# Attention scores with 64 contracted rows: the two row halves by turns, kept together, and one mask product for a whole PSUM bank

## Chip, cores and metric

The kernel runs on one core of a Trainium2 chip. A core has five engines that matter here: TensorE (PE, matrix products, with its weight loads PEld), VectorE (DVE), ScalarE (ACT), GpSimd (POOL) and SyncE (SP, which issues the DMAs). The metric is the device time of one execution in microseconds (us). Lower is better.

## The reference, cut to what matters

Two decoder layers over 256 tokens of width 1024 in float32. Layer 0 mixes differential attention and a Mamba-2 scan, then a SwiGLU. Layer 1 mixes native sparse attention (NSA) and multi-head latent attention (MLA), then eight routed SwiGLU experts of which each token takes two. The change touches the three places where causal attention scores are made:

```python
# layer 0, differential attention: 4 heads, 2 components of 64 dimensions each
sc = jnp.einsum('bqhcd,bkhcd->bhcqk', q_blk, k) * d ** -0.5
p = softmax(where(causal, sc, NEG_INF)); attn = p[:, :, 0] - lam_full * p[:, :, 1]
# layer 1, MLA: 4 heads, each 128 dimensions without and 64 with rotary position
q_full = concatenate([q_nope, q_rope]); k_full = concatenate([k_nope, k_r])
o = causal_attention_blocked(q_full, k_full, v, 192 ** -0.5)
# layer 1, NSA: 2 groups of 4 heads, 64 dimensions; selected and window branch
s_s = einsum('bqgrd,bgqkd->bgrqk', q_blk, k_sel) * scale    # all 4 blocks are selected here
s_w = einsum('bqgrd,bkgd->bgrqk', q_blk, k_win) * scale     # the window covers all tokens
```

Queries are taken in two blocks of 128 (b = 0, 1). Block b sees K = 128 (b + 1) keys, of which the last 128 are masked causally.

## The kernel before

**Stages.** Layer 0's projections, scan, attention and output projection run until some 140 us, its SwiGLU until some 320 us, layer 1's projections and attentions until some 475 us, the routing until some 490 us, and the experts until the end. In the experts 1 MB weight tiles come in through the tiles `raw`, `xres`, `xg`, `more` and `fl`; weights that take part in a split product are divided into a high part `wh` and a rest `wl` (ACT or DVE makes `wh`, DVE makes `wl`), and `mm3` multiplies by them in three products (the lines 498, 499 and 500 of the profile).

**What sets the order.** All code outside the SwiGLU's and the experts' loops is recorded by `Recorder` and put into an order by a list scheduler: `flush` runs it with four settings (`WAYS`) and keeps the order with the shortest planned end. Each recorded operation has an engine (or two to choose from, `flex` and `either`), a planned duration (`pe_cost` and its like), and predecessors by the regions that it reads and writes. A new duration or a new operation anywhere can thus move every other operation of the same flush. There are two flushes: layer 0 up to the first SwiGLU chunk, and from the last SwiGLU chunk to the first experts' gather. The loops of the SwiGLU and of the experts are written out in program order. Recorded operations stand in the profile under the line of the proxy's call, 312 (317 in the loops).

**Scores.** A score tile `ps` is one PSUM bank of 512 columns (`pa()`, a ring of eight). `sp[0]` and `sp[1]` hold two 256-column halves each (`i`, or `br` in NSA). The operands of component or group 0 lie in partitions 0 to 63, those of component or group 1 in 64 to 127, so the products for `sp[0]` use the upper half of TensorE's rows and those for `sp[1]` the lower half. These products are plain float32, and each shows in the trace as two passes (two weight loads, two matmuls). `mask_add` adds the causal mask as a product of `identr` and `negmr`, both fp32r, one pass of 128 columns for each of the two halves of a bank. Then `softmax_exp` takes a maximum of the bank on DVE (`nm`) and two exponentials on ACT, `probs_T` transposes the result on PE, and products with the values follow. Ahead of the change every one of these products is an operation of its own, which the scheduler places freely.

In differential attention there are 16 such 64-row products (8 for each query block), in MLA 8 (the rotary part, after a 128-row product for the rest), in NSA 32.

Of the kernel before, what the change touches and what calls it, by code (L numbers as in the profile page):

```python
# [2 lines left out]

# [1 line left out]

# [14 lines left out]
P = 128  # L20
# [33 lines left out]
BIG = 4  # L54
HALFP = 64
LAG = 3
LATE, AFTER, HALF = 1, 2, 3
EXPLN = "natural_log_exp_and_others"
SILU = "silu_and_others"
# [8 lines left out]
class Recorder:  # L68
# [14 lines left out]
            (0.035, 2.357, 18.415, 0.5, 15.484, 17.49))  # L83

    def __init__(self):
        self.on, self.late = False, 0
        self.rings, self.ring_of, self.held = {}, {}, {}
        self.reset()

# [20 lines left out]
    def add(self, alts, outs, ins, table=None):  # L110
        o = _Op()
        o.i, o.alts, o.preds, o.succs, o.allocs = len(self.ops), alts, set(), [], []
        o.late = self.late
        rr = [r for r in map(self.region, ins) if r is not None]
        ww = [r for r in map(self.region, outs) if r is not None]
        o.touch = {r[0] for r in rr + ww}
        o.start = max((t for r in rr for lo, hi, t in self.when.get(r[0], ()) if lo < r[4] and r[3] < hi), default=0.0)
        for n in o.touch:
            if n in self.ring_of and n not in self.wr and n not in self.held:
                o.allocs.append(n)  # L120
                self.first[n] = o.i
            elif n in self.first:
                o.preds.add(self.first[n])
            self.wr.setdefault(n, [])
            self.rd.setdefault(n, [])
        pe = alts[0][0] == "PE"

        def hits(lst, r):

            for j, q, qpe in lst:  # L130
                if (q[1] < r[2] and r[1] < q[2] and q[3] < r[4] and r[3] < q[4]) or (pe and qpe and r[5]):
                    yield j

        for r in rr:
            o.preds.update(hits(self.wr[r[0]], r))
        for r in ww:
            o.preds.update(hits(self.wr[r[0]], r))
            o.preds.update(hits(self.rd[r[0]], r))
        for r in rr:
            self.rd[r[0]].append((o.i, r, pe))  # L140
        for r in ww:
            self.wr[r[0]].append((o.i, r, pe))
        if table == "load":
            o.preds.update(self.since)
            self.since = []
            if self.fence is not None:
                o.preds.add(self.fence)
            self.fence = o.i
        elif table == "use":
            if self.fence is not None:  # L150
                o.preds.add(self.fence)
            self.since.append(o.i)
        self.ops.append(o)

    def hold(self, tiles):
        self.held.update({ap.tensor.name: True for ap in tiles if ap.tensor.name in self.ring_of})
# [147 lines left out]
class Proxy:  # L304
# [9 lines left out]
    def __getattr__(self, fn):  # L314
        def call(*args, table=None, **kw):
            if not self.rec.on:
                return getattr(self.eng, fn)(*args, **kw)  # L317
            outs, ins = operands(args, kw)
            self.rec.add([self.alt(fn, args, kw)], outs, ins, table)
        return call  # L320


# [53 lines left out]
def kernel(ctx: ExitStack, tc: tile.TileContext, a, out: bass.AP):  # L376
    nc = tc.nc
    rec = Recorder()
# [127 lines left out]
    def mmx(o, l, r, start, stop):  # L506
        T.matmul(o, l, r, start=start, stop=stop, skip_group_check=True)
# [103 lines left out]
            flex(dstT[:, :, b * P:(b + 1) * P], tp.rearrange("p (i t) -> p i t", i=4))  # L611
        return f

    def mask_add(ps):
        mmx(ps, identr, negmr, False, True)

    def softmax_exp(s2, pr, sums):

# [6 lines left out]
    def v2(t, K):  # L625
        return t.rearrange("p (c k) -> p c k", c=2)[:, :, :K]
# [336 lines left out]
    for b in range(2):  # L963
        K = P * (b + 1)
        ops = pa()
        for hp_ in range(2):
            sp = [pa() for c in range(2)]
            for i in range(2):
                for c in range(2):
                    mmx(sp[c][:, i * 256:i * 256 + K], qT[c * 64:(c + 1) * 64, 2 * hp_ + i, b * P:(b + 1) * P],  # L970
                        kT[c * 64:(c + 1) * 64, 2 * hp_ + i, 0:K], i == 0, False)
            prs, sms = [], []
            for c in range(2):
                for i in range(2):
                    mask_add(sp[c][:, i * 256 + b * P:i * 256 + K])
                pr = v2(tw(), K)
                sums = small([P, 2], "sums")
                softmax_exp(v2(sp[c], K), pr, sums)
                prs.append(pr)
                sms.append(sums)  # L980
                V.reciprocal(sums, sums)
            V.tensor_scalar(sms[1], sms[1], nlam, None, op0=OP.mult)
            for i in range(2):
                V.tensor_scalar(prs[1][:, i, :], prs[1][:, i, :], sms[1][:, i:i + 1], None, op0=OP.mult)
                V.scalar_tensor_tensor(prs[0][:, i, :], prs[0][:, i, :], sms[0][:, i:i + 1], prs[1][:, i, :],
                                       op0=OP.mult, op1=OP.add)
            pt = probs_T(prs[0], b)
            for i in range(2):
                h = 2 * hp_ + i
                for j in range(b + 1):  # L990
                    o = (i * (b + 1) + j) * P
                    mmx(ops[:, h * P:(h + 1) * P], pt[:, o:o + P], v_sb[:, j, h * P:(h + 1) * P], j == 0, j == b)
            cs = slice(hp_ * 256, (hp_ + 1) * 256)
            on = norm_heads(ops[:, cs].rearrange("p (h d) -> p h d", d=P), 2, P)
            mx = mixt[b][0][:, cs]
            V.tensor_tensor(mx.rearrange("p (h d) -> p h d", d=P), on, bc(gsub[:, None, :], [P, 2, P]), OP.mult)
            mp.feat(0, b, 2 * hp_, mx)
# [213 lines left out]
    for b in range(2):  # L1211
        K = P * (b + 1)
        ts = slice(b * P, (b + 1) * P)
        ops = pa()
        sp = [pa() for c in range(2)]
        for i in range(2):
            for c in range(2):
                h = 2 * i + c
                o = sp[c][:, i * 256:i * 256 + K]
                mmx(o, qnT[:, h, ts], knT[:, h, 0:K], i == 0, False)  # L1220
                mmx(o, qrT[64 * c:64 * c + 64, i, ts], krT[64 * c:64 * c + 64, 0:K], False, False)
                mask_add(sp[c][:, i * 256 + b * P:i * 256 + K])
        sums = small([P, 2, 2], "sums4")
        for c in range(2):
            pr = v2(tw(), K)
            softmax_exp(v2(sp[c], K), pr, sums[:, :, c])
            pt = probs_T(pr, b)
            for i in range(2):
                h = 2 * i + c
                for j in range(b + 1):  # L1230
                    o = (i * (b + 1) + j) * P
                    mmx(ops[:, h * P:(h + 1) * P], pt[:, o:o + P], vm[:, j, h * P:(h + 1) * P], j == 0, j == b)
        sf = sums.rearrange("p i c -> p (i c)")
        V.reciprocal(sf, sf)
        V.tensor_tensor(mixt[b][1].rearrange("p (h d) -> p h d", d=P), ops.rearrange("p (h d) -> p h d", d=P),
                        bc(sf[:, :, None], [P, 4, P]), OP.mult)
# [10 lines left out]
    for b in range(2):  # L1247
# [26 lines left out]
        sums = small([P, 4, 2, 2], "nsums")  # L1274
        for r in range(4):
            sp = [pa() for g in range(2)]
            for br in range(2):
                for g in range(2):
                    mmx(sp[g][:, br * 256:br * 256 + K], qT[64 * g:64 * g + 64, r, ts], ksT[br][64 * g:64 * g + 64, 0:K],
                        br == 0, False)  # L1280
            for g in range(2):
                for br in range(2):
                    mask_add(sp[g][:, br * 256 + b * P:br * 256 + K])
                pr = v2(tw(), K)
                softmax_exp(v2(sp[g], K), pr, sums[:, r, g])
                pt = probs_T(pr, b)
                cs = slice((2 * r + g) * 64, (2 * r + g + 1) * 64)
                for br in range(2):
                    for j in range(b + 1):
                        o = (br * (b + 1) + j) * P  # L1290
                        mmx(ops[br][:, cs], pt[:, o:o + P], vn[:, j, br * P + g * 64:br * P + g * 64 + 64], j == 0, j == b)
            fs = small([P, 2, 2], "nfs")
            V.reciprocal(fs, sums[:, r].rearrange("p g c -> p c g"))
            V.tensor_tensor(fs, fs, gates[:, b, 1:3, r, :], OP.mult)
            for br in range(2):
                for g in range(2):
                    oh_ = obv[:, 2 * r + g, :]
                    V.scalar_tensor_tensor(oh_, ops[br][:, (2 * r + g) * 64:(2 * r + g + 1) * 64], fs[:, br, g:g + 1], oh_,
                                           op0=OP.mult, op1=OP.add)
            mp.feat(0, b, r, ob[:, r * P:(r + 1) * P])  # L1300
# [493 lines left out]
```

## Time and profile before

| | us |
|---|---|
| median of 3 timed runs | 1177.9 (1177.27 to 1180.31) |
| the profiled execution's own time | 1181.26 |
| its span in the trace | 1179.5 |
| busy: PE, weight loads, DVE, ACT | 1152.2, 843.8, 718.6, 602.6 |

The profiled execution is 3.4 us above the median of the timed runs, and its span is 1.8 us short of its own time. A matmul's duration in the trace reaches past the start of the next one, so what a product takes of TensorE's time is read from start to start.

### The profile page before, as it was taken

To read this page: it belongs to the slowest core of one execution; us is meant where nothing else is said; L and a number is where in the kernel's file an instruction comes from. 1 tells how busy PE (TensorE), PEld (TensorE's weight loads), DVE (VectorE), ACT (ScalarE), POOL (GpSimd) and SP (SyncE) were. 2 spreads that over 40 slices of the span, in tenths; PEclk is the share of its full clock that TensorE was granted. 3 is DMA by queue.
4 is the path that set the end of the run, shared out by engine and by line. 5 is a ranking of instruction groups with operands and counts; after the bars stand their busy time and mean duration, and the time that the engine had idled before them with its cause. 6 is when DMAs were issued, how large, how long until landed. Compare 5 with 4: busy or idle time off the path is not lost.

```text
span 1179.5 us, 16563 instructions
## 1 busy us (share of the span) xinstructions
PE 1152.2 (98%) x6171; PEld 843.8 (72%) x6171; DVE 718.6 (61%) x1179; ACT 602.6 (51%) x1015; POOL 28.6 (2%) x59
## 2 busy tenths in 40 slices
PE   6999999999999999999999999999999999999997
PEld 6887888888777878876666666666666666666663
DVE  5999945444389765784555665556565546565542
ACT  5767743444388565564445444445445554444431
POOL 1040000000300000000000000000000000000000
PEclk9999999999999999799999999999999999999999
DMA  9443455556353513378999999999999999999994
GB/s 353 153 177 108 144 213 179 181 181 225 107 175 131 208 55 134 134 291 356 387 393 417 399 411 394 405 423 421 380 415 411 408 395 402 418 409 422 416 413 164
DMA packets 52069, 348.13 MB, mean 295 GB/s; under 512 B 5904, under 2 KB 6032, under 8 KB 11536
## 3 DMA queue, kind: packets, MB, share of 16 engines
q1 hardware_dynamic: 51984, 347.02, 74.6%
q8 instruction: 50, 0.82, 0.3%
q14 instruction: 35, 0.29, 0.1%
HBM read 345.95 MB, written 1.05 MB: 294 GB/s over the span
## 4 chain that ended last, share of the span: by engine, by line
PE 83%; DMA 8%; DVE 4%; ACT 3%; issue 2%; SPq 0%; DVEq 0%; ACTq 0%
PE ps L317 21%; PE ps L498 17%; PE ps L500 17%; PE ps L499 17%; PE ps L312 11%; DMA raw<-in_moe_dram 3%; ACT wh L317 2%; DVE wl L317 2%; DMA fl<-in_moe_dram 2%; DMA xg<-in_moe_dram 1%; DMA more<-in_moe_dram 1%; ACT tw L312 1%; DMA raw<-in_w_dram 1%; DMA xres<-in_moe_dram 1%; DVE wl L312 0%
## 5 line engine op out<-in xcount | busy, mean ns | idle before, releaser
L317 DVE TENSOR_TENSOR wl<-raw,wh 128x2048 fp32r<-128x2048 f32 x90 | 206.3, 2293 | 160.7 <-ACT wh L317 160.7
L317 ACT ACTIVATE wh<-raw 128x2048 fp32r<-128x2048 f32 x90 | 172.0, 1911 | 118.1 <-DMA raw<-in_moe_dram 63.9
L498 PE MATMUL ps<-wh,fh 128*128 128x512 f32 (+2 forms) x544 | 221.5, 407 | 0.0
L499 PE MATMUL ps<-wl,fh 128*128 128x512 f32 (+2 forms) x544 | 211.3, 388 | 0.0
L500 PE MATMUL ps<-wh,fl 128*128 128x512 f32 (+2 forms) x368 | 142.2, 387 | 0.0
L317 ACT ACTIVATE tw<-ps 128x128 f32<-128x128 f32 (+2 forms) x114 | 43.3, 388 | 180.0 <-PE ps L317 178.0
L498 PEld LDWEIGHTS ps<-wh,fh 128*128 128x128 f32 x544 | 103.2, 190 | 20.6 <-ACT tw L312 0.3
L498 PE MATMUL ps<-wh,tw 128*128 128x512 f32 (+1 forms) x276 | 113.9, 413 | 1.7 <-ACT tw L317 1.0
L499 PEld LDWEIGHTS ps<-wl,fh 128*128 128x128 f32 x544 | 103.1, 190 | 17.3
L500 PE MATMUL ps<-wh,tw 128*128 128x512 f32 (+1 forms) x276 | 109.0, 395 | 0.0
L499 PE MATMUL ps<-wl,tw 128*128 128x512 f32 (+1 forms) x276 | 108.9, 395 | 0.0
L312 DVE TENSOR_TENSOR wl<-raw,wh 128x512 fp32r<-128x512 f32 (+1 forms) x149 | 98.9, 679 | 2.9 <-ACT wh L312 2.8
L317 DVE TENSOR_TENSOR tw<-ps,tw 128x256 fp32r<-128x256 f32 (+1 forms) x70 | 35.9, 521 | 91.8 <-ACT tw L317 91.6
L312 ACT ACTIVATE wh<-raw 128x512 fp32r<-128x512 f32 (+1 forms) x135 | 77.7, 623 | 19.7 <-PE ps L500 16.1
L317 PE MATMUL ps<-raw,xs 128*64 128x256 f32 x720 | 87.2, 384 | 0.0
L500 PEld LDWEIGHTS ps<-wh,fl 128*128 128x128 f32 x368 | 69.1, 188 | 14.8 <-DVE fl L312 0.7
L498 PEld LDWEIGHTS ps<-wh,tw 128*128 128x128 f32 x276 | 51.8, 188 | 28.1 <-issue 15.4
L498 PE MATMUL ps<-wh,xg 128*128 128x512 f32 x176 | 71.0, 403 | 0.0
L500 PE MATMUL ps<-wh,fh 128*128 128x512 f32 x176 | 69.8, 396 | 0.0
L317 PEld LDWEIGHTS ps<-raw,xs 128*64 128x64 f32 x720 | 48.4, 136 | 29.8 <-issue 8.5
L500 PE MATMUL ps<-wh,xg 128*128 128x512 f32 x176 | 69.3, 394 | 0.0
L499 PE MATMUL ps<-wl,xg 128*128 128x512 f32 x176 | 68.7, 390 | 0.0
(295 smaller groups left out, 1807.3 us busy)
## 6 DMA issues: line engine op xcount, KB each, us to landing
raw<-in_moe_dram SPq DMA_DIRECT2D x131, 1024.0 KB, 9.3
xg<-in_moe_dram SPq DMA_DIRECT2D x33, 1024.0 KB, 8.9
xres<-in_moe_dram SPq DMA_DIRECT2D x33, 1024.0 KB, 8.3
more<-in_moe_dram SPq DMA_DIRECT2D x32, 1024.0 KB, 8.7
fl<-in_moe_dram SPq DMA_DIRECT2D x32, 1024.0 KB, 8.6
raw<-in_ffn_dram SPq DMA_DIRECT2D x30, 1024.0 KB, 4.8
raw<-in_w_dram SPq DMA_DIRECT2D x23, 1024.0 KB, 5.2
raw<-in_ffn_dram SPq DMA_DIRECT2D x12, 256.0 KB, 3.8
```

The lines of the kernel that those rows point to most:

```text
L312: return (self.name, self.cost(fn, args, kw), lambda: real(*args, **kw))
L317: return getattr(self.eng, fn)(*args, **kw)
L498: nc.tensor.matmul(ps, xh, wh, start=start, stop=False)
L499: nc.tensor.matmul(ps, xh, wl, start=False, stop=False)
L500: nc.tensor.matmul(ps, xl, wh, start=False, stop=stop)
```

## The change

A context manager `rec.together(share)` collects all recorded calls inside it into one operation of one engine, whose planned duration is the sum of theirs times `share`. The 64-row score products of a pair of banks and the two mask products go into such a bundle, in the order `sp[0]`, `sp[1]`, `sp[0]`, `sp[1]`, mask, mask, with a share `PAIRED = 0.65`. `mask_add` takes the whole bank now: one product of 2 x 128 moving columns (the same 128 mask columns twice) in place of two products of 128. In MLA the four 128-row products go ahead of the bundle. The 56 score products stay, in 14 bundles of four (4 in differential attention, 2 in MLA, 8 in NSA); of 56 mask products 28 are left.

```diff
@@ -1,5 +1,5 @@
 import math
-from contextlib import ExitStack
+from contextlib import ExitStack, contextmanager
 
 import numpy as np
 
@@ -54,6 +54,7 @@
 BIG = 4
 HALFP = 64
 LAG = 3
+PAIRED = 0.65
 LATE, AFTER, HALF = 1, 2, 3
 EXPLN = "natural_log_exp_and_others"
 SILU = "silu_and_others"
@@ -83,7 +84,7 @@
             (0.035, 2.357, 18.415, 0.5, 15.484, 17.49))
 
     def __init__(self):
-        self.on, self.late = False, 0
+        self.on, self.late, self.bundle = False, 0, None
         self.rings, self.ring_of, self.held = {}, {}, {}
         self.reset()
 
@@ -151,6 +152,19 @@
                 o.preds.add(self.fence)
             self.since.append(o.i)
         self.ops.append(o)
+
+    @contextmanager
+    def together(self, share=1.0):
+
+        if not self.on:
+            yield
+            return
+        self.bundle = []
+        yield
+        calls, self.bundle = self.bundle, None
+        e, = {c[0][0] for c in calls}
+        self.add([(e, share * sum(c[0][1] for c in calls), lambda: [c[0][2]() for c in calls])],
+                 [o for c in calls for o in c[1]], [i for c in calls for i in c[2]])
 
     def hold(self, tiles):
         self.held.update({ap.tensor.name: True for ap in tiles if ap.tensor.name in self.ring_of})
@@ -316,7 +330,10 @@
             if not self.rec.on:
                 return getattr(self.eng, fn)(*args, **kw)
             outs, ins = operands(args, kw)
-            self.rec.add([self.alt(fn, args, kw)], outs, ins, table)
+            if self.rec.bundle is not None:
+                self.rec.bundle.append((self.alt(fn, args, kw), outs, ins))
+            else:
+                self.rec.add([self.alt(fn, args, kw)], outs, ins, table)
         return call
 
 
@@ -611,8 +628,9 @@
             flex(dstT[:, :, b * P:(b + 1) * P], tp.rearrange("p (i t) -> p i t", i=4))
         return f
 
-    def mask_add(ps):
-        mmx(ps, identr, negmr, False, True)
+    def mask_add(ps, b):
+
+        mmx(v2(ps, 256)[:, :, b * P:(b + 1) * P], identr, bc(negmr[:, None, :], [P, 2, P]), False, True)
 
     def softmax_exp(s2, pr, sums):
 
@@ -965,14 +983,15 @@
         ops = pa()
         for hp_ in range(2):
             sp = [pa() for c in range(2)]
-            for i in range(2):
+            with rec.together(PAIRED):
+                for i in range(2):
+                    for c in range(2):
+                        mmx(sp[c][:, i * 256:i * 256 + K], qT[c * 64:(c + 1) * 64, 2 * hp_ + i, b * P:(b + 1) * P],
+                            kT[c * 64:(c + 1) * 64, 2 * hp_ + i, 0:K], i == 0, False)
                 for c in range(2):
-                    mmx(sp[c][:, i * 256:i * 256 + K], qT[c * 64:(c + 1) * 64, 2 * hp_ + i, b * P:(b + 1) * P],
-                        kT[c * 64:(c + 1) * 64, 2 * hp_ + i, 0:K], i == 0, False)
+                    mask_add(sp[c], b)
             prs, sms = [], []
             for c in range(2):
-                for i in range(2):
-                    mask_add(sp[c][:, i * 256 + b * P:i * 256 + K])
                 pr = v2(tw(), K)
                 sums = small([P, 2], "sums")
                 softmax_exp(v2(sp[c], K), pr, sums)
@@ -1216,10 +1235,14 @@
         for i in range(2):
             for c in range(2):
                 h = 2 * i + c
-                o = sp[c][:, i * 256:i * 256 + K]
-                mmx(o, qnT[:, h, ts], knT[:, h, 0:K], i == 0, False)
-                mmx(o, qrT[64 * c:64 * c + 64, i, ts], krT[64 * c:64 * c + 64, 0:K], False, False)
-                mask_add(sp[c][:, i * 256 + b * P:i * 256 + K])
+                mmx(sp[c][:, i * 256:i * 256 + K], qnT[:, h, ts], knT[:, h, 0:K], i == 0, False)
+        with rec.together(PAIRED):
+            for i in range(2):
+                for c in range(2):
+                    mmx(sp[c][:, i * 256:i * 256 + K], qrT[64 * c:64 * c + 64, i, ts], krT[64 * c:64 * c + 64, 0:K], False,
+                        False)
+            for c in range(2):
+                mask_add(sp[c], b)
         sums = small([P, 2, 2], "sums4")
         for c in range(2):
             pr = v2(tw(), K)
@@ -1274,13 +1297,14 @@
         sums = small([P, 4, 2, 2], "nsums")
         for r in range(4):
             sp = [pa() for g in range(2)]
-            for br in range(2):
+            with rec.together(PAIRED):
+                for br in range(2):
+                    for g in range(2):
+                        mmx(sp[g][:, br * 256:br * 256 + K], qT[64 * g:64 * g + 64, r, ts],
+                            ksT[br][64 * g:64 * g + 64, 0:K], br == 0, False)
                 for g in range(2):
-                    mmx(sp[g][:, br * 256:br * 256 + K], qT[64 * g:64 * g + 64, r, ts], ksT[br][64 * g:64 * g + 64, 0:K],
-                        br == 0, False)
+                    mask_add(sp[g], b)
             for g in range(2):
-                for br in range(2):
-                    mask_add(sp[g][:, br * 256 + b * P:br * 256 + K])
                 pr = v2(tw(), K)
                 softmax_exp(v2(sp[g], K), pr, sums[:, r, g])
                 pt = probs_T(pr, b)
```

The scheduler makes the following of it. TensorE, at the start of differential attention: `ps_302`/`ps_303` are the pair of banks of the first bundle (query block 0), `ps_339`/`ps_340` that of block 1; the even-c bank (302, 339) takes rows 0 to 63 and the other rows 64 to 127. Before:

```order
L312 MATMUL ps_302<-kT_199,qT_198 128x128
L312 MATMUL ps_340<-kT_199,qT_198 128x256
L312 MATMUL ps_303<-negmr_108,identr_107 128x128
L312 MATMUL ps_302<-kT_199,qT_198 128x128
L312 MATMUL ps_303<-negmr_108,identr_107 128x128
L498 MATMUL ps_268<-wh_262,fh_89 128x512
L499 MATMUL ps_268<-wl_263,fh_89 128x512
L500 MATMUL ps_268<-wh_262,fl_90 128x512
L312 MATMUL ps_340<-kT_199,qT_198 128x256
L312 MATMUL ps_339<-kT_199,qT_198 128x256
```

and in the changed kernel:

```order
L326 MATMUL ps_302<-kT_199,qT_198 128x128
L326 MATMUL ps_303<-kT_199,qT_198 128x128
L326 MATMUL ps_302<-kT_199,qT_198 128x128
L326 MATMUL ps_303<-kT_199,qT_198 128x128
L326 MATMUL ps_302<-negmr_108,identr_107 128x2x128
L326 MATMUL ps_303<-negmr_108,identr_107 128x2x128
L326 MATMUL ps_339<-kT_199,qT_198 128x256
L326 MATMUL ps_340<-kT_199,qT_198 128x256
```

The 64-row products and the masks, which stood between 128-row products one or two at a time, now stand in one piece for each pair of banks.

TensorE in NSA, where the pair of query block 1 for the first head of each group is made (`ps_3228`/`ps_3229` before, `ps_3227`/`ps_3228` after; `more` holds the queries and `xg1` the keys; `cp` with `tw` is a transpose of probabilities). Before:

```order
L312 MATMUL ps_3176<-xg1_2876,more_2872 128x128
L312 MATMUL ps_3228<-xg1_2876,more_2872 128x256
L312 MATMUL ps_3176<-xg1_2876,more_2872 128x128
L312 MATMUL ps_3228<-xg1_2876,more_2872 128x256
L312 MATMUL ps_3176<-negmr_108,identr_107 128x128
L312 MATMUL ps_3167<-cp_86,tw_3165 128x128 x2
L312 MATMUL ps_3228<-negmr_108,identr_107 128x128
```

and after:

```order
L326 MATMUL ps_3227<-xg1_2875,more_2871 128x256
L326 MATMUL ps_3228<-xg1_2875,more_2871 128x256
L326 MATMUL ps_3227<-xg1_2875,more_2871 128x256
L326 MATMUL ps_3228<-xg1_2875,more_2871 128x256
L326 MATMUL ps_3227<-negmr_108,identr_107 128x2x128
L326 MATMUL ps_3228<-negmr_108,identr_107 128x2x128
L326 MATMUL ps_3166<-cp_86,tw_3164 128x128 x2
```

Here the order before already had, by chance of the schedule, two banks of opposite row halves by turns (3176 is a lower-half bank, 3228 an upper-half one); in the changed kernel every pair stands so.

VectorE at the start of differential attention, with the maxima `nm` of the first banks. Before:

```order
L312 TENSOR_REDUCE nm_309<-ps_303 128x2
L312 TENSOR_TENSOR rs_t2_282<-rs_r2_280 128x2
L312 TENSOR_TENSOR wl_377<-raw_375,wh_376 128x512
L312 SCALAR_TENSOR_TENSOR rs_t2_282<-rs_t2_282,rs_v2_281 128x2
L312 TENSOR_TENSOR wl_377<-raw_375,wh_376 128x512
L312 TENSOR_REDUCE nm_306<-ps_302 128x2
```

and after:

```order
L326 TENSOR_REDUCE nm_309<-ps_303 128x2
L326 TENSOR_REDUCE nm_306<-ps_302 128x2
L326 TENSOR_SCALAR rs_v2_281<-ss2_278 128x2
L326 TENSOR_TENSOR rs_t2_282<-rs_r2_280 128x2
L326 TENSOR_TENSOR wl_293<-raw_291,wh_292 128x512
L326 TENSOR_REDUCE nm_346<-ps_340 128x2
```

The two maxima of a pair stand next to each other, since both banks become ready together; the splits of weights (`wl`) that stood between them come behind. The order of the other operations of both flushes moves too, from the first projections on.

## Rows read from the trace of the kernel before

**Rows 1.** The page: span, and busy time of TensorE; the chain's shares.

```profile
PE 1152.2 (98%) x6171; PEld 843.8 (72%) x6171; DVE 718.6 (61%) x1179; ACT 602.6 (51%) x1015; POOL 28.6 (2%) x59
PE 83%; DMA 8%; DVE 4%; ACT 3%; issue 2%; SPq 0%; DVEq 0%; ACTq 0%
```

**Rows 2.** Stretches: busy PE, PEld, DVE, ACT, POOL; granted clock, DMA share, GB/s.

```profile
95.00:140.00 45.00, 44.88 (x238) 34.98 (x236) 40.85 (x114) 31.94 (x98) 0.00 (x0) 1.00 0.42 147
...
400.00:460.00 60.00, 59.38 (x359) 46.27 (x359) 37.94 (x109) 32.12 (x108) 0.00 (x0) 1.00 0.25 86
...
475.00:490.00 15.00, 13.35 (x53) 12.52 (x54) 11.34 (x59) 4.62 (x11) 0.00 (x0) 0.50 0.32 105
...
545.00:1100.00 555.00, 553.87 (x3012) 367.92 (x3011) 319.64 (x291) 268.05 (x309) 0.00 (x0) 1.00 0.99 406
```

**Rows 3.** TensorE's longest wait for another engine: us in total, times, longest.

```profile
PE ps L312 <- ACT wh L312: 8.7, 2, 7.1
```

**Rows 4.** Groups of TensorE's products by form: count, busy us, mean ns of one.

```profile
L312 PE MATMUL ps<-negmr,identr 128*128 128x128 f32 x56 | 14.0, 291 | 0.0
...
L499 PE MATMUL ps<-wl,fh 128*128 128x256 f32 x16 | 4.5, 281 | 0.0
```

**Rows 5.** TensorE in order of time; first and last of 37 pieces of 64-row products.

```profile
98.28 0.71 PE L312 MATMUL ps<-kT,qT 64*128 64x128 f32 x4
...
452.62 0.70 PE L312 MATMUL ps<-xg,more 64*128 64x256 f32 x2
```

**Rows 6.** The same view; two 256-column products of one row half.

```profile
108.16 1.13 PE L312 MATMUL ps<-kT,qT 64*128 64x256 f32 x4
109.22 0.50 PE L498 MATMUL ps<-wh,fh 128*128 128x512 f32 x1
```

**Rows 7.** The same view, 101.3 to 106.3 us.

```profile
101.40 0.48 PE L312 MATMUL ps<-kT,qT 64*128 64x128 f32 x2
101.81 0.33 PE L312 MATMUL ps<-negmr,identr 128*128 128x128 f32 x1
101.98 0.44 PE L498 MATMUL ps<-wh,fh 128*128 128x512 f32 x1
102.26 0.39 PE L499 MATMUL ps<-wl,fh 128*128 128x512 f32 x1
102.49 0.40 PE L500 MATMUL ps<-wh,fl 128*128 128x512 f32 x1
102.82 0.70 PE L312 MATMUL ps<-kT,qT 64*128 64x256 f32 x4
103.45 0.44 PE L312 MATMUL ps<-negmr,identr 128*128 128x128 f32 x2
103.82 0.70 PE L312 MATMUL ps<-kT,qT 64*128 64x256 f32 x2
104.44 0.33 PE L312 MATMUL ps<-cp,z_sb 128*128 128x128 f32 x1
...
105.41 0.71 PE L312 MATMUL ps<-kT,qT 64*128 64x128 f32 x4
106.04 0.44 PE L312 MATMUL ps<-negmr,identr 128*128 128x128 f32 x2
```

**Rows 8.** The same view in NSA: four products, two of each row half.

```profile
414.97 1.13 PE L312 MATMUL ps<-xg,more 64*128 64x128 f32 x8
416.04 0.33 PE L312 MATMUL ps<-negmr,identr 128*128 128x128 f32 x1
```

**Rows 9.** Groups of DVE's operations, 95 to 140 us.

```profile
L312 DVE TENSOR_TENSOR wl<-raw,wh 128x512 fp32r<-128x512 f32 x25 | 16.6, 684 | 0.0
```

**Rows 10.** The chain that ended last: start, us, what.

```profile
117.35 2.43 PE ps L312 x22
...
457.41 0.61 DVE nm L312
...
462.88 1.07 PE ps L312 x8
```

## The prediction

> **What bounds the kernel now.** I read the page first. TensorE is busy for 98% of the span and holds 83% of the chain that ended last, DMA only 8% [rows 1]. Busy time overstates a pipelined engine, so I looked at the waits next: the largest entry is 8.7 us for ACT in two places, 7.1 us of it at once [rows 3], and no other entry is over 2.8 us. By stretches, the stage with differential attention (95 to 140 us) and the one with NSA (400 to 460 us) run with TensorE full and at the upper clock (1.00, 2.4 GHz), while DMA moves little (share 0.42 and 0.25) [rows 2]. DVE is nearly full in the first (40.85 of 45 us) and has room in the second (37.94 of 60 us), ACT has room in both. So a product less on TensorE ends these stages earlier, until DVE or a softmax's latency takes over.
>
> The experts (545 to 1100 us) run at a DMA share of 0.99 [rows 2]. They don't swallow the gain: their first weights are loaded while NSA still runs and the share is 0.25, so this stage begins earlier by what is saved ahead of it and lasts as long as before.
>
> **Score products in bundles.** The order of time on TensorE gives each case a price, from the first product's start to the start of the next 128-row product.
> - One 64-row product alone: 0.41 us with 128 moving columns (101.40 to 101.81), 0.62 us with 256 (103.82 to 104.44) [rows 7].
> - Two of one row half in a row: 0.63 us with 128 columns (105.41 to 106.04) [rows 7], 1.06 us with 256 (108.16 to 109.22) [rows 6].
> - Two of 256 columns and opposite halves: 0.63 us (102.82 to 103.45) [rows 7], no more than one alone. The halves do run at once.
> - Two and two by turns, which is the order of a bundle: 1.07 us for all four (414.97 to 416.04) [rows 8], what the longer half needs alone. There one half has 128 columns and the other 256; with 256 in both I expect the same, by the opposite pair above.
>
> Before, the 56 score products (by the code 16 in differential attention, 8 in MLA and 32 in NSA, half of each with 256 columns) stand in 37 pieces from 98.28 to 452.62 us [rows 5]: 8 alone at 0.41, 13 alone at 0.62, 7 pairs of one half at 0.63, 5 at 1.06, 2 opposite pairs at 0.63, one piece of three products (0.64) and the one of four (1.07). That is 3.3 + 8.1 + 4.4 + 5.3 + 1.3 + 0.6 + 1.1 = 24.1 us. After, there are 14 bundles. The 7 of query block 0 (128 columns) should take what two of one half take, 0.63 us, and the 7 of block 1 take 1.07 us: 4.4 + 7.5 = 11.9 us. **Saved: 12.2 us.**
>
> **Changes between 64-row and 128-row products.** Ahead of a piece the last 128-row product holds TensorE longer: 0.33 us (102.49 to 102.82) against 0.23 (102.26 to 102.49) [rows 7]. The first one behind a piece does so too: 0.17 us (101.81 to 101.98) [rows 7] against 0.11 for a plain short product (2.43 us for 22) [rows 10]. A piece thus costs 0.10 + 0.06 us besides its own time, and 23 pieces fewer save **3.7 us**.
>
> **Masks.** 56 products of 128 columns [rows 4] become 28 of 256. One plain short product costs 0.11 us. A 256-column mask isn't in the trace. Below, it costs the same 0.11, above, the 0.23 of a 512-column product. I take 0.12, since an fp32r product of 256 columns in a projection lasts 281 ns and a mask of 128 columns 291 [rows 4]: it is no longer. Saved: 56 x 0.11 - 28 x 0.12 = **2.8 us** (it would be 0 at 0.23).
>
> TensorE's work falls by 12.2 + 3.7 + 2.8 = 18.7 us: by about 4.5 in differential attention (9 pieces and 16 masks become 4 bundles), 4 in MLA, 10 in NSA.
>
> **What is taken back.** The scheduler's whole order moves. In differential attention DVE has 40.85 us of work in a stage that would need 40.5 us of TensorE. If DVE can be kept 95% full, the stage lasts 43.0 us, and 2.5 of the 4.5 us are lost; if splits of weights (25 of 0.68 us, 16.6 us in all [rows 9]), some of them for the SwiGLU's first weights, slide behind it, nothing is. I take half, 1.2 us. In NSA the same work leaves DVE 76% full (37.94 of 50 us), which is no bound, but the end of NSA is a chain: the last maximum starts at 457.41 and its results reach TensorE at 462.88 [rows 10], 5.5 us that don't shrink. TensorE now reaches that point with less other work left to cover it; I take a third of it, 1.5 us. The bundle also makes a pair's first maximum wait for the whole pair, up to 0.6 us of latency per bundle, which lies beside 128-row products as long as there are some. Net: 18.7 - 2.7 = **16.0 us**.
>
> The profiled execution took 1181.26 us, so one like it would take 1165.3. The median of the timed runs is 3.4 us lower (1177.9), and the predicted median is 1177.9 - 16.0 = **1162 us**. Its own range goes from all of the 18.7 us kept plus a little luck of the order (1157) to a loss three times as large as I take (1167).
>
> **A rule that speaks against it.** In these rows the engine behind TensorE is not late: of 45 and 60 us, DVE and ACT leave 4 to 28 us free [rows 2]. The Trainium skill, "TensorEngine Tiling (Array Packing)", section "Performance Considerations", says that tiling speeds up TensorE but not the emptying of PSUM, which may become the bottleneck. By that rule the gain in differential attention and MLA would be the time until DVE is full, and the result that of the first rival below. The trace so far agrees only for differential attention, where DVE is 91% full.
>
> **Rivals.**
> 1. *Softmax takes over.* DVE and ACT, not TensorE, end the attention stages. For it: 40.85 of 45 us on DVE, and the 5.5 us chain. Against it: NSA, with half of the gain, has DVE at 63% now. Price: differential attention gives 2 of 4.5, MLA 2 of 4, NSA 5 of 10: 9 us, 1169.
> 2. *The halves don't overlap in bundles*, so the change doesn't do what it says. Eight passes in a row would cost 0.63 + 0.63 less one change of 0.17 = 1.09 us for 128 columns, and 1.06 + 1.06 - 0.2 = 1.92 for 256: 7 x 3.0 = 21.1 us against 24.1. With 3.7 and 2.8 that is 9.5 us, less the same 2.7: 1171. Against it: the four at 414.97 [rows 8].
> 3. *The bundles stall TensorE's queue: slower.* TensorE works in order, and a bundle needs two free banks of eight and all its operands at once. A softmax takes 5.5 us from its maximum to its return to TensorE at 462.88 [rows 10], and if TensorE stood at a bundle for one such turnaround until banks come free, five stalls would cost 27.5 us: 1177.9 - 18.7 + 27.5 = 1187. It decides from the fifth of 14. For it: before, a single product could fill a gap, a bundle can't. Against: the order puts bundles of the two query blocks next to each other, not two of one, and TensorE's waits in these stages are near nothing today.
> 4. *The new order is luckier elsewhere.* The rest of both flushes is reordered too, and could lose a part of the waits there or of the stretch at the lower clock (475 to 490 us at 0.50, 1.2 GHz [rows 2]), which routing brings about and which I leave as it is: 1157.
>
> **Chances.** Forecast 0.66, softmax bound 0.18, no overlap 0.04, stalls 0.03, luckier 0.07, and 0.02 for no net change. Faster by over 0.3% (3.5 us, about what a measurement tells from no change) holds for all but the stalls and a far tail of the softmax case: 0.94; the same 0.03, slower 0.03. The range that holds 8 in 10 takes in the luckier case and most of the softmax case: 1156 to 1170.
>
> **What the new profile would show.** 14 pieces of 64-row products, 0.63 us long with 128 columns and 1.07 with 256, right: the overlap. Pieces of 1.1 and 1.9 us: rival 2. Mask pairs that take 0.34 us from first start to the next product behind them (0.17 + 0.12 and some): right; 0.5 us: the mask price was wrong. Layer 0's SwiGLU starting 3 to 4.5 us earlier and the routing 15 to 17 us earlier: the sum; new entries among TensorE's waits for `nm`, `tw` or `wl` in these stages: rivals 1 and 3. The experts' stage should last as long as before; if it grows by what was saved, DMA bounds it from an earlier point than I think. The prediction is wrong if the lower clock appears within the attentions, if a chain of softmax steps of over 8 us stands in them, or if TensorE waits for a bundle's banks.

## The result, and the profile after

The changed kernel takes 1164.5 us (median of 4 runs, 1162.6 to 1166.3). The kernel before, on the same chip, takes 1177.9 (4 runs). The ratio of the runs is 0.9872, with a 95% interval of 0.9858 to 0.9887: 15.1 us saved (13.3 to 16.7). A later set (`after_again`, below) gave 0.9866 (0.9849 to 0.9884). The forecast was 1162 us and 16.0 us saved.

From here on a gain in us is (ratio - 1) x 1179 us, 1179 being about what the kernel before took on the chips used. One execution's span says less: the experts' stage, whose instructions are the same in all of these kernels, varies between the profiled executions by up to 4.1 us (from its first product to the last it lasted 685.5 us in the profile shown here, and 683.2 in a second profile of the same kernel).

The page of the profile after: busy time by engine, and the chain that ended last. TensorE is busy 18.8 us less than in [rows 1], and holds a larger share of the chain.

```profile
PE 1133.4 (97%) x6143; PEld 833.2 (72%) x6143; DVE 720.7 (62%) x1185; ACT 601.2 (52%) x1016; POOL 28.7 (2%) x59
PE 89%; DMA 5%; DVE 3%; ACT 1%; issue 1%; SPq 0%; DVEq 0%; ACTq 0%
```

Stretches after, with the columns of [rows 2]: differential attention, MLA's end and NSA, routing, experts.

```profile
95.00:140.00 45.00, 44.97 (x247) 35.78 (x247) 43.29 (x124) 34.94 (x109) 0.00 (x0) 1.00 0.43 155
...
380.00:440.00 60.00, 57.20 (x392) 46.21 (x391) 48.02 (x137) 37.21 (x129) 0.00 (x0) 1.00 0.34 124
...
459.50:476.50 17.00, 14.66 (x56) 13.53 (x57) 11.20 (x59) 4.70 (x11) 0.00 (x0) 0.50 0.34 121
545.00:1100.00 555.00, 552.88 (x3005) 367.30 (x3005) 319.96 (x289) 268.57 (x307) 0.00 (x0) 1.00 0.99 407
```

In differential attention DVE went from 40.85 to 43.29 of 45 us, and TensorE still doesn't wait (44.97). In the attentions of layer 1 TensorE is no longer full (57.20 of 60 us): here something is taken back. Experts and the slow stretch of the routing look as before.

TensorE in order of time after, the first bundles (start, us, what). Each bundle stands in one row of eight passes, and the two masks behind it in the next.

```profile
98.70 0.39 PE L517 MATMUL ps<-wh,fl 128*128 128x512 f32 x1
99.02 0.71 PE L326 MATMUL ps<-kT,qT 64*128 64x128 f32 x8
99.67 0.51 PE L326 MATMUL ps<-negmr,identr 128*128 128x256 f32 x2
100.10 1.13 PE L326 MATMUL ps<-kT,qT 64*128 64x256 f32 x8
101.17 0.50 PE L326 MATMUL ps<-negmr,identr 128*128 128x256 f32 x2
101.51 0.40 PE L515 MATMUL ps<-wh,fh 128*128 128x512 f32 x1
```

From start to start, the four products of 128 columns take 0.65 us (99.02 to 99.67), those of 256 take 1.07 (100.10 to 101.17), and two wide masks take 0.34 (101.17 to 101.51). All 14 bundles together last 12.2 us: seven of 0.645, six of 1.064, and one, in NSA, of 1.26 (414.52 to 415.77), whose second half starts 0.2 us behind the first:

```profile
414.52 1.33 PE L326 MATMUL ps<-xg,more 64*128 64x256 f32 x8
415.77 0.51 PE L326 MATMUL ps<-negmr,identr 128*128 128x256 f32 x2
```

What it waits for stands in the single records: the first weight load of the second half waits for ScalarE's copy of a transpose out of a PSUM bank, and its product starts 0.04 us behind the end of this copy. ScalarE in order of time after:

```profile
414.27 0.39 ACT L326 ACTIVATE tw<-ps 128x256 f32<-128x256 f32 x1
```

So this bundle stands for a bank for 0.2 us, too short for the view of waits (which bank it is, the trace leaves out). In e3_no_turns, which has the same order, it happens again behind the same copy.

Where the time came from is read from three landmarks in both traces. They are the first product of the SwiGLU's second projection in layer 0, the first product of the routing (`m`, with what it waited for), and the first of the experts. Before:

```profile
162.28 0.40 PE L498 MATMUL ps<-wh,tw 128*128 128x512 f32 x1
...
475.83 0.60 PE L312 MATMUL ps<-m,tw 128*128 128x8 f32 x2 [1.78 <-DVE m L312]
...
486.19 0.77 PE L498 MATMUL ps<-wh,fh 128*128 128x512 f32 x1
```

After:

```profile
158.25 0.40 PE L515 MATMUL ps<-wh,tw 128*128 128x512 f32 x1
...
461.03 0.59 PE L326 MATMUL ps<-m,tw 128*128 128x8 f32 x2 [2.53 <-DVE m L326]
...
471.38 0.77 PE L515 MATMUL ps<-wh,fh 128*128 128x512 f32 x1
```

Layer 0 gives 4.0 us, layer 1's attentions 10.8 more, and from the routing on everything stands 14.8 us earlier, to the end. The experts have moved as a block.

What was taken back shows among TensorE's waits in layer 1's attentions. The view of waits, 320 to 440 us, before (engine, line, waited for: us in total, times, longest):

```profile
PE ps L312 <- DVE rs_t L312: 2.0, 2, 1.8
PE ps L498 <- ACT tw L312: 0.7, 1, 0.7
PE ps L312 <- DVE more L312: 0.5, 1, 0.5
PE ps L312 <- ACT tw L312: 0.2, 1, 0.2
```

The same view and stretch after:

```profile
PE ps L326 <- DVE tw L326: 3.4, 5, 1.7
PE ps L326 <- DVE xres L326: 1.3, 2, 0.7
PE ps L326 <- DVE more L326: 1.0, 2, 0.7
PE ps L326 <- ACT tw L326: 0.3, 1, 0.3
```

That is 6.0 us in place of 3.4, nearly all of it for DVE, and in many short waits. None of these listed waits stands at a bundle.

### The profile page after: what moved, and what is told of

It reads as the page before. It is cut to its first block, busy times and chain, and to the rows that moved or that the text cites. A ratio compares the mean times of both kernels' runs of the same rounds, so it can differ in the third digit from the quotient of the medians.

```text
span 1164.5 us, 16524 instructions
## 1 busy us (share of the span) xinstructions
PE 1133.4 (97%) x6143; PEld 833.2 (72%) x6143; DVE 720.7 (62%) x1185; ACT 601.2 (52%) x1016; POOL 28.7 (2%) x59
## 4 chain that ended last, share of the span: by engine, by line
PE 89%; DMA 5%; DVE 3%; ACT 1%; issue 1%; SPq 0%; DVEq 0%; ACTq 0%
PE ps L331 24%; PE ps L515 19%; PE ps L517 18%; PE ps L516 18%; PE ps L326 10%; DMA raw<-in_moe_dram 2%; DMA fl<-in_moe_dram 1%; ACT wh L331 1%; DVE wl L326 1%; DMA raw<-in_w_dram 1%; DMA more<-in_moe_dram 1%; DVE wl L331 1%; DVE xres L331 0%; DVE tw L326 0%; DVE tw L331 0%
## 5 line engine op out<-in xcount | busy, mean ns | idle before, releaser
L326 ACT ACTIVATE wh<-raw 128x512 fp32r<-128x512 f32 (+1 forms) x130 | 74.8, 628 | 18.2 <-PE ps L517 10.0
L515 PEld LDWEIGHTS ps<-wh,tw 128*128 128x128 f32 x276 | 51.9, 188 | 26.8 <-issue 15.4
```

Of the source, the lines that this page charges most:

```text
L326: return (self.name, self.cost(fn, args, kw), lambda: real(*args, **kw))
L515: nc.tensor.matmul(ps, xh, wh, start=start, stop=False)
```

## The experiments

Eleven runs on three chips, each beside runs of the kernel before. Two questions were asked: which part of the change gives how much, and how much of a difference comes from the order that the scheduler lays out when any planned duration changes. So some kernels keep the order of all other instructions, instruction by instruction on each engine, and change only what is issued at a place; others let the scheduler lay out a new one.

| run | order | ratio to before (95%) | us |
|---|---|---|---|
| the change | new | 0.9872 (0.9858 to 0.9887) | -15.1 |
| after_again | the change's | 0.9866 (0.9849 to 0.9884) | -15.8 |
| e3_no_turns | the change's | 0.9870 (0.9853 to 0.9887) | -15.3 |
| f2_two_masks_same_order | the change's | 0.9893 (0.9877 to 0.9908) | -12.6 |
| f4_halves_apart | the change's | 0.9984 (0.9975 to 0.9993) | -1.9 |
| f1_wide_old_order | of before | 0.9963 (0.9950 to 0.9976) | -4.4 |
| e1_mask_only | another | 1.0012 (1.0002 to 1.0021) | +1.4 |
| e2_two_masks | another | 0.9947 (0.9927 to 0.9967) | -6.2 |
| e4_masks_twice | another | 0.9941 (0.9924 to 0.9959) | -7.0 |
| share_05 | another | 0.9893 (0.9878 to 0.9909) | -12.6 |
| share_08 | another | 0.9945 (0.9929 to 0.9961) | -6.5 |
| share_10 | another | 0.9924 (0.9911 to 0.9938) | -9.0 |

The first three rows have one order and, as will be seen, one cost: their mean, -15.4 us, is what the others are compared with.

### One part alone, or one part undone, with the order left to the scheduler

**e1_mask_only**: the kernel before, with `mask_add` of the change, its calls adapted, and nothing else.

```diff
-    def mask_add(ps):
-        mmx(ps, identr, negmr, False, True)
+    def mask_add(ps, b):
+        mmx(v2(ps, 256)[:, :, b * P:(b + 1) * P], identr, bc(negmr[:, None, :], [P, 2, P]), False, True)
```

> The kernel before with one alone of the three parts: one 256-column mask product for each bank in place of two of 128 columns, no bundles. The theory (TensorE's time in the attentions counts fully, and a mask product of 256 columns costs about what one of 128 did): 28 products of 0.11 us fewer, 2 to 3 us faster than before, about 1175.5. Rival (the wider product costs twice the narrow one, so that only the bundles gained): within 0.5 us of before. Rival (the new time comes from a changed order of all instructions, not from the parts): anything between -6 and +6 us.

**e2_two_masks**: the change, with the masks alone undone.

```diff
-        mmx(v2(ps, 256)[:, :, b * P:(b + 1) * P], identr, bc(negmr[:, None, :], [P, 2, P]), False, True)
+        for i in range(2):
+            mmx(ps[:, i * 256 + b * P:i * 256 + (b + 1) * P], identr, negmr, False, True)
```

> The changed kernel with the masks alone undone: two 128-column products for each bank again, inside the bundles. The theory: 28 more products of 0.11 us, 2.5 to 3.5 us slower than the changed kernel, so about 1167.5, and 10 to 12.5 us faster than before. Rival (the softmax chains set the pace of the attentions now): within 1 us of the changed kernel.

**e4_masks_twice**: the change, with the line of `mask_add` in a loop of two. The mask is added twice.

> The changed kernel with each mask product issued twice, which adds 28 products of 256 columns to TensorE in the attentions and no work to any other engine. The theory (TensorE's time there still counts fully): 28 times 0.11 to 0.12 us, so 3 to 3.5 us slower than the changed kernel, about 1168. Rival (the softmax chains on VectorE and ScalarE have taken over as the limit): under 1 us slower, since the added products go into idle time of TensorE.

All three missed. Wide masks alone gained nothing (+1.4 us). Two narrow masks, or two wide ones, cost 9.2 and 8.4 us beside the change where 3 were expected. No theory had these sizes; only the last rival of e1_mask_only, a changed order, left room for its miss. By the products' own time the theory is right, though: summed over TensorE's order of time in the attentions, from each product's start to the next, scores, masks and changes of row count take 36.9 us before, 34.7 in e1_mask_only, 18.4 after, 21.5 in e2_two_masks and 23.0 in e4_masks_twice. The rest came from elsewhere. Since these edits change planned durations, a new order was laid out in each, and this was the suspect for the next four.

### The same edits with the order held

**f1_wide_old_order**: the kernel before. The first mask of a bank is recorded as before and issues nothing, the second is recorded as before and issues the wide product.

```diff
...
+        def wide():
+            nc.tensor.matmul(v2(bank, 256)[:, :, b * P:(b + 1) * P], identr, bc(negmr[:, None, :], [P, 2, P]), **kw)
+
+        rec.add([(e, cost, wide if i else lambda: None)], [ps], [identr, negmr])
```

> The kernel before, every instruction in its old order, with the mask products alone changed: the first one of a bank left out and the second one widened to 256 columns, without the planner being told. The theory (TensorE's time in the attentions counts fully; the run with wide masks only was no faster because its planner laid out another order): 28 products fewer, 2 to 2.8 us faster than before. Rival (a wide mask costs what two narrow ones do, or the softmax chains set the pace): within 0.7 us of before.

**f2_two_masks_same_order**: the change. Recorded as one wide product with its planned duration, two narrow ones are issued.

```diff
...
+        def both():
+            for i in range(2):
+                nc.tensor.matmul(o[:, i], identr, negmr, **kw)
+
+        rec.bundle.append(((e, cost, both), [o], [identr, m2]))
```

> The changed kernel, every instruction in its order, with two mask products of 128 columns issued in each place of one of 256. The theory (TensorE-bound, the rest of the 8 us that two masks cost with a new order was the order's): 2.5 to 3.2 us slower than the changed kernel. Rival (the two masks themselves cost 8 us): 7 to 9 us slower. Rival (the softmax chains set the pace): under 1 us slower.

With the order held, the masks behave as the theory has them. Wide ones gain 4.4 us (2.8 to 5.9) in the old order, narrow ones cost 2.8 in the new one. The 4.4 is more than the 2.1 by which TensorE's products shrink in that trace. A piece of the rest is a short stretch at the lower clock, below, which the profile of before has and that of this run has not; it is worth about 1.7 us, and with it 3.8 us lie within the interval.

**f4_halves_apart**: the change, with one edit in each of the three bundles, by which a 128-row mask parts the two halves.

```diff
             with rec.together(PAIRED):
-                for br in range(2):
-                    for g in range(2):
+                for g in range(2):
+                    for br in range(2):
                         mmx(sp[g][:, br * 256:br * 256 + K], qT[64 * g:64 * g + 64, r, ts],
                             ksT[br][64 * g:64 * g + 64, 0:K], br == 0, False)
-                for g in range(2):
-                    mask_add(sp[g], b)
+                    mask_add(sp[g], b)
```

> The changed kernel, every other instruction in its order, but inside each bundle the two products and the mask of one half stand ahead of those of the other, so that a 128-row mask parts the halves and they cannot run at once: 28 pieces in place of 14. The theory (the gain is the overlap and the fewer changes, all on the path): 7 bundles by 1.26 + 0.16 - 0.65 and 7 by 2.12 + 0.16 - 1.07, together 13.9 us slower than the changed kernel, so about 1178, no faster than before by more than 1. Rival (the halves' overlap is partly beside the softmax chains): 5 to 9 us slower. Rival (most of the gain came from the new order around the bundles): under 4 us slower.

Measured: 13.5 us slower than the change (its own ratio, -1.9, against the mean of -15.4), with 13.9 expected. TensorE in order of time in this run, three of the four pieces that the first two bundles fall into:

```profile
97.48 0.71 PE L326 MATMUL ps<-kT,qT 64*128 64x128 f32 x4
98.12 0.39 PE L326 MATMUL ps<-negmr,identr 128*128 128x256 f32 x1
98.44 0.71 PE L326 MATMUL ps<-kT,qT 64*128 64x128 f32 x4
99.08 0.39 PE L326 MATMUL ps<-negmr,identr 128*128 128x256 f32 x1
99.39 1.13 PE L326 MATMUL ps<-kT,qT 64*128 64x256 f32 x4
100.45 0.39 PE L326 MATMUL ps<-negmr,identr 128*128 128x256 f32 x1
```

Two products of one half take 0.64 us (97.48 to 98.12) and 1.06 (99.39 to 100.45), what all four of a bundle take together after. The products, their count and the order around them are the same, and nearly the whole gain is gone. Of the 14.3 us by which TensorE's time grows in this trace, 11.5 are the score products (12.2 to 23.7 us), which is the overlap; the rest comes with the 14 more changes of row count. Since the loss is 13.5 of these 14.3 us, a microsecond on TensorE in the attentions is still nearly a microsecond at the end. The softmax engines, which would have hidden it, are not the bound.

**e3_no_turns**: the change, with the loops exchanged as in the diff above and the masks left behind all four products, in all three bundles.

> The changed kernel with the order inside each bundle alone changed: the two products of the lower row half first, then the two of the upper, in place of by turns. Theory A (TensorE takes the products in the order of the program, and a product can only start beside the one ahead of it where that one is on the other half): the two halves overlap only in the middle, a bundle of 128-column products takes about 0.85 to 0.9 us in place of 0.645 and one of 256 columns about 1.7 in place of 1.06, so that 5 to 6.5 us of the gain are lost: about 1170. Rival B (being kept together is what counts, and the halves find their overlap whatever the order): bundles of 0.65 and 1.07 us, within 1 us of the changed kernel.

Theory A fell. The time is that of the change (-15.3 us), and so are the bundles:

```profile
100.02 0.72 PE L326 MATMUL ps<-kT,qT 64*128 64x128 f32 x8
100.67 0.51 PE L326 MATMUL ps<-negmr,identr 128*128 128x256 f32 x2
101.11 1.14 PE L326 MATMUL ps<-kT,qT 64*128 64x256 f32 x8
```

They take 0.65 us again (100.02 to 100.67). In the single records of the trace the second half starts 13 ns behind the first, where it is 7 ns with the turns, and then both go on side by side. (The records don't name the half. But two products of one half alone start their passes at 0, 213, 325 and 437 ns, and the eight passes here fall into two such rows, the second one 13 ns later.) So a product of the second half overtakes the one of the first half that stands ahead of it in the program. To be kept together is what counts, not the turns.

### The planner's number

Only `PAIRED` differs here: the planned duration of a bundle, 0.5, 0.8 or 1.0 of the sum in place of 0.65.

```diff
-PAIRED = 0.65
+PAIRED = 0.5
```

> The changed kernel with one number of the planner changed: a bundle is planned at the full sum of its products' costs instead of 0.65 of it. The instructions are the same, only their order differs. The theory that the order by itself is worth several us: between 3 and 8 us away from the changed kernel, on either side, with bundles of the same 0.65 and 1.07 us. Rival (the order is worth little, and the run with two masks lost its 8 us otherwise): within 1.5 us of the changed kernel.

> The changed kernel with a bundle planned at 0.5 of its products' costs instead of 0.65; the instructions are the same, in another order. The theory that the order by itself is worth several us either way: 1 to 6 us away from the changed kernel. In the run with 1.0 the loss came with TensorE's waits in NSA and with two short stretches at the lower clock; if these are the cause, the time here follows the sum of TensorE's waits and those stretches, whichever sign it has.

> The changed kernel with a bundle planned at 0.8 of its products' costs. As for 0.5: 1 to 6 us away from the changed kernel, by TensorE's waits and the short stretches at the lower clock; if a right price of the bundle matters to the planner rather than luck, the times of 0.5, 0.65, 0.8 and 1.0 lie on a curve with one lowest point; if it is luck, they lie in no order.

> The changed kernel once more, beside the runs of the planner's number, so that they are compared on one chip: 1163 to 1167 us, 14 to 16 us faster than before.

The instructions are the same, and the time is 2.8, 8.9 and 6.4 us longer (0.5, 0.8, 1.0); 0.8 missed its range of 1 to 6. These lie on no curve with one lowest point: 0.8 is worse than 1.0. So the number 0.65 is worth several us, by the order that happened to come out. None of the runs beat the change.

Two things go with a slow order. One is TensorE's waits: share_10 has one of 4.0 us and share_08 one of 4.3, both for DVE, longer than any in the attentions after. The other is short stretches at the lower clock (0.50, 1.2 GHz). Windows of before, share_10 (two stretches) and f1_wide_old_order, one fence each; the clock is the third number from the end:

```profile
370.00:380.00 10.00, 8.06 (x50) 7.14 (x49) 9.70 (x41) 9.10 (x32) 0.00 (x0) 0.83 0.29 105
374.20:377.60 3.40, 3.40 (x15) 3.01 (x14) 3.35 (x17) 3.23 (x11) 0.00 (x0) 0.50 0.00 0
```

```profile
370.00:380.00 10.00, 7.97 (x55) 7.70 (x56) 8.80 (x37) 8.80 (x26) 0.00 (x0) 0.83 0.00 0
420.00:430.00 10.00, 7.79 (x49) 6.14 (x48) 8.75 (x25) 8.15 (x32) 0.00 (x0) 0.83 0.66 246
```

```profile
370.00:380.00 10.00, 7.98 (x58) 6.96 (x58) 9.93 (x45) 9.63 (x35) 0.00 (x0) 1.00 0.30 105
```

Before, TensorE stood still for 1.8 us, and 3.4 us at half speed followed soon after, which cost about 1.7 us (half of the stretch, an estimate). In share_10 there are two such stretches, in e1_mask_only also two (near 375 and near 445 us, the second of 6.8 us), and in the change not at all before the routing. The mean granted clock over all runs of a kernel goes the same way: 0.991 for the change (4 runs), 0.990 for before (11 runs on the same chip), 0.988 for e1_mask_only and share_10, 0.987 for share_08.

How much of the times these two account for can be counted from the records. The table gives, in us, the change of TensorE's time for scores and masks; the change of its listed waits, from 95 us to the first product of the routing (5.2 us before, 9.2 after); and an estimate for the clock, the difference of the mean granted clocks of all runs (0.9897 before, 0.9912 for the change) times the span.

| run (its mean clock), against | products | waits | clock | sum | measured |
|---|---|---|---|---|---|
| the change (0.9912), before | -18.5 | +4.0 | -1.8 | -16.3 | -15.4 |
| e1_mask_only (0.9883), before | -2.2 | +2.9 | +1.7 | +2.4 | +1.4 |
| e2_two_masks (0.9879), the change | +3.1 | +2.5 | +3.9 | +9.5 | +9.2 |
| e4_masks_twice (0.9887), the change | +4.6 | +2.4 | +2.9 | +9.9 | +8.4 |
| share_05 (0.9896), the change | +0.6 | +0.3 | +1.9 | +2.8 | +2.8 |
| share_08 (0.9872), the change | +0.5 | +4.3 | +4.7 | +9.5 | +8.9 |
| share_10 (0.9875), the change | +0.3 | +2.7 | +4.3 | +7.3 | +6.4 |

All sums lie within 1.5 us of what was measured, and for the four runs with a held order within 1.2. So what the first three runs left open is waits and clock. This is a count over records: no edit changed the waits or the clock alone. (In the share runs, the 0.3 to 0.6 us of products are bundles with a late half, like the one above.)

## Why the prediction was right

**The score products.** Forecast: from 24.1 to 11.9 us by bundles of 0.63 and 1.07. Measured: 24.2 to 12.2 us, by 0.645 and 1.064 and the one bundle with a late half. That halves side by side cost what one costs alone was rightly taken from four products of before [rows 8] and two opposite pairs [rows 7]. That it holds for all 14 was not sure; f4_halves_apart shows that it is this overlap which carries the gain, 13.5 us together with the changes of row count.

**Changes of row count and masks.** Forecast 3.7 + 2.8 = 6.5 us. From start to start they went from 12.7 to 6.2 us, so 6.5. The two masks take 0.34 us, as forecast, and 0.5 would have meant that a wide one costs two narrow ones. The masks' part alone is 2.8 us in the new order (f2_two_masks_same_order).

**The sum on TensorE.** Forecast 18.7, measured 36.9 - 18.4 = 18.5 us.

**What is taken back.** Forecast 2.7 us, 1.2 of it in differential attention because DVE would be full there, 1.5 in the chain at the end of NSA (named as a third of 5.5 us, which is 1.8). The size was too small and most of it came elsewhere. In layer 0, 4.5 us of products were saved, and the SwiGLU landmark came 4.0 us earlier: 0.5 was taken back. From the first product of differential attention (98.28 before [rows 5], 99.02 after) to the landmark the time shrank by 4.8 us, but three 512-column products of 0.23 us each went ahead of that first product, so this says the same. DVE, at 96%, was just able to keep up. The wait at the routing grew only from 1.78 to 2.53 us. But between, in MLA and NSA, TensorE waits for DVE in many places. Layer 1 lost 14.0 us of products and gained 10.8. The stretch at the lower clock that went is worth 1.7 more, so about 5 us were taken back here (14.0 + 1.7 - 10.8). From the SwiGLU landmark to the routing the listed waits grew from 5.2 to 9.2 us, which is 4.0 of it; where the last us lies isn't shown. The waits are the order's rather than the bundles': f4_halves_apart, with 10 us more work for TensorE there and the same order, still has 8.6 us of them, the longest wait for `tw` again 1.7 us.

**The net.** Forecast 16.0, measured 15.1: a term of 2.7 that was about 5.5, against a gain of 1.7 that was left out. That these two partly cancel is luck, and the close number owes something to it.

**The rivals.** The first (softmax takes over, 9 us) is refuted by f4_halves_apart, though waits of TensorE for DVE are most of what was taken back: they stay when TensorE gets more to do, so they don't come from softmax being the bound. The second (no overlap) is refuted by every bundle. f4_halves_apart makes it happen by force, and ends at -1.9 us; the forecast for it was -6.8, with fewer changes of row count. The third (bundles stall TensorE's queue) happened once and in small: one bundle's second half stood 0.2 us for a bank, and no other bundle's row carries a wait. The fourth (a luckier order) happened in part, by the 1.7 us of the clock, at another place than was named.

**The signs.** Pieces of 0.65 and 1.07 us, mask pairs of 0.34 and a SwiGLU 4.0 us earlier came as announced. The routing moved by 14.8 us, just short of the 15 to 17. `tw` and `xres` are new among the waits, which was to speak for rivals 1 and 3 and, as f4_halves_apart shows, need not. The lower clock within the attentions, named as a sign of being wrong, was there before the change already (374.2 to 377.6 us) and was overlooked.

**The rule on PSUM.** The Trainium skill, "TensorEngine Tiling (Array Packing)", section "Performance Considerations", says that tiling doesn't speed up the emptying of PSUM. This trace agrees only in that DVE came to 96% in differential attention and 0.5 of 4.5 us was taken back there. By that rule the next step of this kind there would gain little, which no run here shows.

**What stays open.** When a pause brings the lower clock: in f1_wide_old_order TensorE stands still for the same 1.8 us at the same place as before, and the clock stays at 1.00. And why an order has more waits than another: the planner's number moved them, but none of the runs shows by which step.

## What to carry to other kernels

Where TensorE bounds a stage and products contract 64 rows, put the products of both row halves next to each other with nothing of 128 rows between: two halves cost what one costs, and each piece less saves the change of row count too. Price such an edit from start to start on TensorE, in rows that already show the pattern. And where a scheduler lays out the order, repeat a small edit with the order held before believing its time: the same masks gave +1.4 us with a new order and -4.4 with the old one.

## What was not expected of the hardware

The order of products inside a bundle makes no difference (0.65 us either way, the second half 13 ns behind instead of 7), while the prediction's third rival had TensorE work in order. The Trainium skill, "TensorE: Matmul & The Clock Gate", section "The mechanism", says that matmuls start in program order without reordering. In e3_no_turns the trace doesn't agree: the third product of the program, on the other row half, starts 13 ns behind the first, and so ahead of the second, which starts 0.33 us behind the first, after the first one's two passes.

The other surprise is the price of an order. With the same instructions it was up to 8.9 us (0.5 to 1.0 for one planned duration), more than half of what the change gains.
